# First layer: experts' outputs added to tokens by indirect DMAs, and late modulation blocks put into the routing

## The chip, the cores and the metric

The kernel runs on one core of a Trainium2 chip. The metric is the device time of one execution in microseconds; where several executions were timed, their median stands for the kernel. TensorE multiplies, VectorE and ScalarE work on what it leaves in PSUM, GpSimd does the indirect transfers, and SyncE issues the plain ones. Each engine takes its own instructions in order.

## The reference

Two blocks of a network follow each other on 512 tokens of width 1024. The first block has two layers. Each computes a mixer (convolutions and attention) and then experts; in the first layer 256 context tokens take the same way as the 512 tokens, in the second they are only read. What matters here is the expert part of the first layer:

```
h2    = rms_norm(x, n2) * (1 + sc2) + sh2          # scales and shifts: "modulation", c @ ada_w + ada_b
probs = softmax(h2 @ router)                       # 16 experts
for each expert e:                                 # expert choice: the expert picks its tokens
    its 64 tokens (32 context tokens) with the highest probs[:, e], weights g
    y = (silu(h @ w_gate[e]) * (h @ w_up[e])) @ w_down[e]
    out[tokens] += g * y                           # a token can be picked by several experts
x = x + g2 * out                                   # the context: xc = xc + cg2 * outc
```

All is float32. The weights of one expert are 3 x 4 MB, those of a layer's experts 201 MB.

## The kernel before, in words

Tokens stand transposed in SBUF: `xT` is 128 partitions x 8 x 512 (feature within a block, block, token), `xcT` the same for 256 context tokens. Instructions are written in program order; a planner then sets the order on every engine by a priority (program order) and a cost model, puts in the waits, and gives out the buffers of the pools.

`experts(l, ...)` begins at line 1022; `has` is true in the first layer. Its steps:

Weights. A unit is a tile of 128 rows x 1024 columns (512 KB) of one weight of one expert; the units are taken in the order gate 0, up 0, gate 1, down 0, up 1, gate 2, down 1, ... `wload(n)` issues the next n loads from SyncE. In the first layer there are 18 tiles `rawA`, 5 tiles `raw` (slots "W", from a pool that the modulation blocks and the dense weights share) and 2 tiles `rawB`, in turn: 25 units. Each product that has used up a unit issues the load of the next.

Modulation. `ada_gen(l, blocks, ...)` (lines 309 to 333) computes one block of 512 modulation values from four tiles `raw` of `ada_w`: eight matmuls, a copy, four transposes, a reduction into `M[l]`. It loads three of the four tiles of the block after it in advance. Blocks 8 to 11 of layer 1 are run at line 1158, after the routing in program order.

Routing (lines 1078 to 1168). Root mean squares and router logits, a softmax, then the top-k: eight rounds of three VectorE instructions on `D` (lines 1123 to 1127), which give the tokens and weights of all experts. Beside it TensorE transposes all tokens back to rows, ScalarE scales them, and SyncE writes them to `hd` in memory. At the end `tok` and `gidx` (token numbers) and `gcol` (weights) are there.

Experts. `gather(e)` (line 1177) is an indirect transfer from GpSimd: 96 rows of `hd` (64 tokens, 32 context tokens) into `xg`. `xpose` transposes them and applies the modulation. `run_gu("g")`, `act`, `run_gu("u")`, `mul`, `hpose` and `down` are the products of one expert; they are run so that `down(e - 1)` stands between the gate and up products of expert e. A product of a unit is four matmuls into the columns of four quarters of TensorE for the tokens (partitions 32 g to 32 g + 32: two halves of the 64 tokens, two halves of the 1024 output columns) and four for the context (four quarters of the columns).

Scatter. `down` leaves y in PSUM (`yx`, `yc`). It is weighted and split in two parts (`Yx`, `Yc`: a rounded value and the rest, lines 1298 to 1308). After every fourth expert `scatter(qd)` builds one-hot matrices from `iota` and `tA`, `tC` (lines 1315, 1350), multiplies them with the parts (lines 1328, 1355), so that each token's column sums what was picked for it, and adds the result, times g2, to `xT` and `xcT` (lines 1331, 1357). It stands in the middle of the up product of experts 4, 8 and 12. The last group is scattered in two steps: `scatter_x(3, (0,))`, the tokens of experts 12 and 13, after expert 14 (line 1390), and after the last product the tokens of experts 14 and 15 and the context of experts 12 to 15, with the squares that the next layer's norm needs.

Of the kernel before, what the change touches and what calls it, by code (L numbers as in the profile page):

```python
# [134 lines left out]
def main_kernel(ctx, tc, I, out, stop=None, dbg=None, manual=False):  # L135
# [173 lines left out]
    def ada_gen(l, blocks, pl, psp):  # L309
        g, o, n = RO["adab"]  # L310
        for b in blocks:
            ada_load(l, b)
            p = psp.tile([128, 512], F32, name="misc")
            for hf in range(4):
                r = raws.pop(("ada", l, b, hf)).rearrange("p (k c) -> p k c", k=2)
                for i in range(2):
                    q = (hf % 2) * 2 + i
                    T.matmul(p[32 * q:32 * q + 32, :], lhsT=s2[:, hf * 2 + i, :], rhs=r[:, i, :],
                             start=(hf < 2), stop=(hf >= 2))
            if 3 < b < 11 or (l == 1 and b != 7 and b < 11):  # L320
                ada_load(l, b + 1, hfs=range(3))
            sb = pl.tile([128, 512], F32, name="sq")
            A.activation(sb, p, AF.Copy)
            yield
            p = psp.tile([128, 512], F32, name="misc")
            for j in range(4):
                T.transpose(p[:, 128 * j:128 * j + 128], sb[:, 128 * j:128 * j + 128], ident)
            mm = M[l][:, 4 * b:4 * b + 4, :]
            V.tensor_reduce(mm, p.rearrange("p (j q s) -> p j s q", j=4, q=4)[:, :, 0:2, :], axis=AX.X, op=OP.add)
            V.tensor_tensor(mm, mm, cols[:, g, o + 48 * l + 4 * b:o + 48 * l + 4 * b + 4, None].to_broadcast([128, 4, 2]),  # L330
                            op=OP.add)
            yield
# [8 lines left out]
    if True:  # L341
# [680 lines left out]
        def experts(l, rwpA, lg, rbias, a2, nA, nB):  # L1022
# [35 lines left out]

            wload(nA + 5)
            with ExitStack() as es:  # L1060
                dr = pool(es, "dr", space=DRAM)
                mp = pool(es, "mp")
                ps = pool(es, "ps", space=bass.MemoryType.PSUM)
                hd = dr.tile([NT, 1024], F32)
                tok = mp.tile([128, 48], F32)
                gcol = mp.tile([128, 48], F32)
# [6 lines left out]
                with ExitStack() as e2:  # L1073
                    hp = pool(e2, "hp")
                    sqp = pool(e2, "sqp2", 3)
                    psp = Psum(ps, {"tr": 2}, {"misc": "tr"})
                    r = roots(sqp, tok_sums(psp, [stA], NTT), NTT, 1.0 / 1024)

# [25 lines left out]
                    D = hp.tile([80, 256], F32)  # L1104
                    V.tensor_copy(D[:NP], pd[:NP, 0:256])
                    wload(6 if l else 0)

                    for t in range(NTT):
# [7 lines left out]
                        SY.dma_start(hd[t * 128:(t + 1) * 128, :], ht)  # L1116
                    wload(nB - (6 if l else 0))


                    vals = hp.tile([80, 64], F32)  # L1120
                    idx = hp.tile([80, 64], U32)
                    for i in range(8):
# [3 lines left out]
                        if i < 7:  # L1126
                            V.match_replace(out=D[:NP], in_to_replace=v8, in_values=D[:NP], imm_value=-1.0)
                    tg = hp.tile([80, 128], F32)
                    ti = hp.tile([80, 128], F32)
# [25 lines left out]
                    else:  # L1155
                        V.tensor_copy(gidx[0:64, :], tok[0:64, 0:16])
                if has:
                    drain(ada_gen(1, range(8, 12), mp, Psum(ps, {"yx": 1}, {"misc": "yx"})))

# [66 lines left out]

                def run_gu(w, e, mid):
                    px = ps.tile([128, 512], F32, name=("ax" if w == "g" else "ux"))
                    pc = ps.tile([128, 256], F32, name=("ac" if w == "g" else "uc")) if has else None
                    xt = xsT[e]  # L1230
                    for u in range(8):
# [3 lines left out]
                        if u == 3:  # L1235
                            for m in mid:
                                m()
                    acc[w, e] = (px, pc)

# [15 lines left out]
                def hpose(e):  # L1255
# [11 lines left out]
                    hT[e] = h  # L1267

                def down(e):
                    px = ps.tile([128, 512], F32, name="yx")  # L1270
# [12 lines left out]
                    for u in range(8):  # L1283
                        r = wt.pop(("d", e, u))
                        prod(px, pc, e, u, r, lx, lc, u == 0, u == 7)
                        wload(1)

                    if e % 4 == 0:
                        Y["x", 0] = sp.tile([128, 2, 2, 512], F32R, name="Yx", bufs=2)
                        Y["x", 1] = sp.tile([128, 2, 2, 512], F32R, name="Yx", bufs=2)  # L1290
                        if has:
                            Y["c"] = sp.tile([128, 2, 4, 256], F32R, name="Yc", bufs=1)
                    y = Y["x", (e % 4) // 2]
                    for g in range(2):
                        hf = g ^ (e % 2)
# [15 lines left out]
                def onehots(qd, pr):  # L1311
                    ohs = []
                    for hf in range(2):
                        oh = sp.tile([128, 512], F32R, name="oh", bufs=4)
                        V.tensor_scalar(oh, iota, tA[:, hf, 2 * qd + pr:2 * qd + pr + 1], None, op0=OP.is_equal)
# [57 lines left out]
                for e in range(17):  # L1373
# [7 lines left out]
                    if e < 16:  # L1381
                        mid = [lambda: xpose(e + 1)]
                        if e > 0 and e % 4 == 0:
                            mid.append(lambda: scatter(e // 4 - 1))
                        run_gu("u", e, mid)
                        mul(e)
                        gather(e + 2)
                    if e == 14:
                        scatter_x(3, (0,))
# [504 lines left out]
```

## Time and profile before

| | |
|---|---|
| median of 3 executions | 2691.11 us (2687.1 to 2695.84) |
| the profiled execution | 2693.99 us |
| its span in the profile | 2692.1 us |
| TensorE (PE) busy | 2512.2 us, 93% |
| VectorE (DVE) / ScalarE (ACT) / GpSimd (POOL) busy | 1156.3 / 900.7 / 590.2 us |
| routing and experts of the first layer | about 451 to 1110 us of the span |

The profile is one execution on the chip. Times count from the start of the span. PE is a matmul on TensorE, PEld a weight load of it, which overlaps with matmuls. An instruction group reads: engine, line, operation, output<-inputs. A matmul of float32 appears as two records. "x8" counts instructions; in square brackets stands how long the engine was idle before, and who released it.

### The profile page before, as it was taken

How to read it: one execution, taken by the hardware profiler on the slowest of the kernel's cores; microseconds unless marked ns; L12 is line 12 of the kernel's file. 1: busy time of each engine (PE TensorE's matmuls, PEld its weight loads, DVE VectorE, ACT ScalarE, POOL GpSimd, SP SyncE). 2: the span in 40 equal slices, each digit the busy share in tenths (PEclk: the TensorE clock that was granted, in tenths of full speed). 3: DMA queues.
4: the chain of work that ended last, by engine and by line, in shares of the span. 5: the costliest groups of instructions: out<-in, count | busy, mean ns of one | idle time of the engine just before them, and what ended most of it. 6: DMA issues, size and time to landing. Idle time of an engine off the chain costs nothing.

```text
span 2692.1 us, 41575 instructions
## 1 busy us (share of the span) xinstructions
PE 2512.2 (93%) x16527; PEld 1526.5 (57%) x16527; DVE 1156.3 (43%) x2466; ACT 900.7 (33%) x1831; POOL 590.2 (22%) x495
## 2 busy tenths in 40 slices
PE   7999999799999999799979989898899999999997
PEld 4776687344444444577753322122577787888876
DVE  4488853223222232679741101021665555444411
ACT  4544363111221211455532111110552435444322
POOL 3423111000000000434220000000333233444443
PEclk9999999899999999799989999999999999999999
DMA  8455365799998987122089999999421102333321
GB/s 287 128 168 155 124 220 208 265 393 375 361 392 313 392 313 251 52 58 65 28 308 361 399 395 400 399 404 409 127 63 32 40 25 63 94 100 96 93 87 64
DMA packets 319352, 572.57 MB, mean 213 GB/s; under 512 B 36320, under 2 KB 187927, under 8 KB 318519
## 3 DMA queue, kind: packets, MB, share of 16 engines
q1 hardware_dynamic: 311143, 552.01, 57.1%
q0 software_dynamic: 7872, 17.84, 2.7%
q8 instruction: 130, 2.13, 0.3%
q14 instruction: 63, 0.52, 0.1%
q10 hardware_dynamic: 144, 0.08, 0.0%
HBM read 553.60 MB, written 10.49 MB: 210 GB/s over the span
## 4 chain that ended last, share of the span: by engine, by line
PE 69%; DMA 15%; DVE 9%; POOL 2%; issue 2%; ACT 2%; SPq 1%; ACTq 0%; DVEq 0%; POOLq 0%
PE px L473 20%; PE ux L1215 4%; PE ax L1215 4%; PE yx L1215 4%; DMA rawA<-in_w_down_dram 3%; PE g L473 2%; PE y L584 2%; PE tr L1328 2%; PE s L553 2%; PE ac L1220 2%; PE px L475 2%; PE uc L1220 2%; PE yc L1220 2%; DMA rawA<-in_w_up_dram 2%; PE ux L1209 2%
## 5 line engine op out<-in xcount | busy, mean ns | idle before, releaser
L443 POOL TENSOR_TENSOR wl<-raw,wh 128x512 fp32r<-128x512 f32 (+1 forms) x312 | 409.0, 1314 | 971.5 <-ACT wh L442 779.2
L442 ACT ACTIVATE wh<-raw 128x512 fp32r<-128x512 f32 (+1 forms) x312 | 193.5, 625 | 441.5 <-PE px L473 210.9
L473 PE MATMUL px<-hh,wh 128*128 128x512 f32 x768 | 316.3, 413 | 5.8 <-DVE xT L1331 1.8
L473 PE MATMUL px<-hh,wl 128*128 128x512 f32 x768 | 314.1, 409 | 6.9 <-POOL wl L443 6.9
L473 PE MATMUL px<-hl,wh 128*128 128x512 f32 x768 | 315.6, 411 | 4.9 <-DVE hl L1019 3.1
L1299 DVE SCALAR_TENSOR_TENSOR Yx<-yx,gcol,Yx 64x512 fp32r<-64x512 f32 x64 | 48.0, 749 | 501.4 <-ACT Yx L1298 501.4
L1181 POOL DMA_INDIRECT xg<-hd,gidx x32 | 29.3, 914 | 842.0 <-PE tr L1193 785.5
L473 PEld LDWEIGHTS px<-hh,wl 128*128 128x128 f32 x768 | 149.5, 195 | 40.5 <-POOL wl L443 7.6
L473 PEld LDWEIGHTS px<-hh,wh 128*128 128x128 f32 x768 | 149.2, 194 | 40.4 <-issue 6.1
L473 PEld LDWEIGHTS px<-hl,wh 128*128 128x128 f32 x768 | 149.3, 194 | 38.6 <-issue 3.8
L1197 ACT ACTIVATE xt<-tr,mod,a 128x64 f32<-128x64 f32 x256 | 86.3, 406 | 197.0 <-PE tr L1193 192.9
L1298 ACT ACTIVATE Yx<-yx,gcol 64x512 fp32r<-64x512 f32 x64 | 43.7, 682 | 317.8 <-PE yx L1215 158.6
L1243 ACT ACTIVATE sa<-ax 128x512 f32<-128x512 f32 x32 | 19.1, 598 | 353.8 <-PE ax L1215 240.7
L785 DVE SCALAR_TENSOR_TENSOR yT<-ub,cols,yT 128x512 f32<-128x512 f32 (+1 forms) x180 | 126.6, 720 | 0.6
L1215 PE MATMUL ax<-rawA,xt 128*32 128x512 f32 x856 | 122.3, 603 | 0.0
L1215 PE MATMUL ux<-rawA,xt 128*32 128x512 f32 x800 | 118.6, 595 | 0.0
L1209 PE MATMUL ux<-rawA,xt 128*64 128x512 f32 x328 | 87.3, 611 | 8.1 <-DMA rawA<-in_w_up_dram 7.9
L1209 PE MATMUL yx<-rawA,hT 128*64 128x512 f32 x316 | 81.5, 621 | 11.5 <-DMA rawA<-in_w_down_dram 10.6
L1328 PE MATMUL tr<-oh,Yx 128*128 128x512 f32 x256 | 78.9, 434 | 12.0 <-ACT Yx L1298 8.1
L565 PE MATMUL pt<-tab,P 128*128 128x128 f32 x448 | 82.7, 285 | 6.9 <-DVE PT L571 4.3
L1209 PE MATMUL ax<-rawA,xt 128*64 128x512 f32 x316 | 77.5, 611 | 8.4 <-DMA rawA<-in_w_gate_dram 7.8
L1328 PEld LDWEIGHTS tr<-oh,Yx 128*128 128x128 f32 x256 | 45.7, 196 | 60.4 <-DVE xT L1331 23.6
(578 smaller groups left out, 4912.0 us busy)
## 6 DMA issues: line engine op xcount, KB each, us to landing
rawA<-in_w_gate_dram SPq DMA_DIRECT2D x186, 512.0 KB, 9.3
rawA<-in_w_up_dram SPq DMA_DIRECT2D x182, 512.0 KB, 10.2
rawA<-in_w_down_dram SPq DMA_DIRECT2D x151, 512.0 KB, 10.2
raw<-in_ada_w_dram SPq DMA_DIRECT2D x80, 512.0 KB, 5.8
raw<-in_w_down_dram SPq DMA_DIRECT2D x74, 512.0 KB, 7.4
raw<-in_w_gate_dram SPq DMA_DIRECT2D x62, 512.0 KB, 10.1
raw<-in_w_in_dram SPq DMA_DIRECT2D x56, 512.0 KB, 5.2
raw<-in_w_up_dram SPq DMA_DIRECT2D x55, 512.0 KB, 6.7
```

What stands on the lines that cost most here:

```text
L442: A.activation(wh[:, :n], raw[i][:, a:a + n], AF.Copy)
L443: G.tensor_tensor(wl[:, :n], raw[i][:, a:a + n], wh[:, :n].bitcast(F32), op=OP.subtract)
L473: T.matmul(px, lhsT=w[:, k % 4, :], rhs=h[:, k0 + k, 0:512], start=st, stop=sp_)
L475: T.matmul(pc, lhsT=w[:, k % 4, :], rhs=h[:, k0 + k, 512:nt], start=st, stop=sp_)
L553: T.matmul(s[:, :w], lhsT=q, rhs=k, start=(a == 0), stop=(a == len(mm) - 1))
L565: T.transpose(pt[:, (t - a) * 128:(t - a + 1) * 128], P[:, t * 128:(t + 1) * 128], ident)
L785: V.scalar_tensor_tensor(acc[:, j, o:o + n], src, w, acc[:, j, o:o + n], op0=OP.mult, op1=OP.add)
L1197: A.activation(xt[:, kk, 0:64], p[:, k * NX:k * NX + 64], AF.Identity, bias=M[l][:, 24 + kk, 0:1], scale=a2[:, kk, 0:1])
L1209: T.matmul(px[64 * g:64 * g + 64, :], lhsT=lx(u), rhs=w[:, 512 * hf:512 * hf + 512], start=first, stop=last)
L1215: T.matmul(px[32 * g:32 * g + 32, :], lhsT=lx(u)[:, 32 * (g % 2):32 * (g % 2) + 32], rhs=w[:, 512 * hf:512 * hf + 512], start=first, stop= ...
L1220: T.matmul(pc[32 * g:32 * g + 32, :], lhsT=lc(u), rhs=w[:, 256 * q:256 * q + 256], start=first, stop=last)
L1328: T.matmul(p, lhsT=Y["x", pr][:, hl_, hf, c * 128:(c + 1) * 128], rhs=ohs[pr][hf], start=(n == 0), stop=(n == 2 * len(prs) - 1))
```

## The change

In the first layer (`has`), the scaled outputs of an expert go to memory instead of being scattered by matmuls. Two arrays of sums stand in device memory: `sumx`, 1024 rows x 512 (two rows per token, one for each half of the columns), and `sumc`, 1024 rows x 256 (four rows per context token). They are filled with zeros from a tile, by two DMAs from SyncE after the writes to `hd`. `place` holds for each partition and expert the row: 2 * token + half, or 4 * token + quarter.

- `down(e)` for e < 14: ScalarE scales `yx` into one tile `ys`, and an indirect DMA from GpSimd adds its 128 rows of 2 KB to `sumx`. For e < 12 VectorE scales `yc` into `yt`, whose 128 rows of 1 KB are added to `sumc`. The two-part split, the one-hot matrices and the matmuls of these experts fall away.
- The tokens of experts 14 and 15 and the context of experts 12 to 15 go the old way, after the last product.
- The sums are read back by six DMAs from GpSimd (`sums_load`: a tile `rb` of 128 tokens x 1024, two buffers), issued after the up products of experts 13 (context) and 14. `sums_add(n)` transposes half a tile (four transposes) and adds it, times g2, to `xT` or `xcT` (four VectorE instructions). The four calls for the context stand in the up product of expert 15, the eight for the tokens between the units of `down(15)`.
- Modulation blocks 8 to 11 of layer 1 are taken in steps during the routing: block 8 after the copy into `D`, the other three after rounds 2, 4 and 6 of the top-k. Their next block is now loaded in four tiles in advance, not three. The five units in slots "W" are loaded after the routing, not before it, and the fourth tile of block 8 takes their place.

```diff
-                ada_load(l, b + 1, hfs=range(3))
+                ada_load(l, b + 1, hfs=range(4 if l == 1 and b > 7 else 3))
...
-            wload(nA + 5)
+            wload(nA if has else nA + 5)
+            if has:
+                ada_load(1, 8)
...
+                    accs = dr.tile([1024, 512], F32, name="sumx"), dr.tile([1024, 256], F32, name="sumc")
+                    place = mp.tile([128, 2, 16], I32)
+                    part = mp.tile([128, 2, 16], F32)
...
+                    ga = ada_gen(1, range(8, 12), mp, Psum(ps, {"yx": 1}, {"misc": "yx"})) if has else iter(())
...
+                    for _ in steps(ga, 2):
+                        pass
                     wload(6 if l else 0)
...
                     wload(nB - (6 if l else 0))
+                    if has:
+                        zz = sqp.tile([128, 1024], F32, name="ht", bufs=4)
+                        G.memset(zz, 0.0)
+                        for acc_, n in zip(accs, (512, 256)):
+                            SY.dma_start(acc_.rearrange("(p a) c -> p (a c)", p=128).rearrange("p (b c) -> p b c", c=1024),
+                                         zz[:, None, :].to_broadcast([128, n // 128, 1024]))
...
+                        if i in (2, 4, 6):
+                            for _ in steps(ga, 2):
+                                pass
...
+                wload(5 if has else 0)
                 if has:
-                    drain(ada_gen(1, range(8, 12), mp, Psum(ps, {"yx": 1}, {"misc": "yx"})))
+                    for i, n in enumerate((2.0, 4.0)):
+                        V.scalar_tensor_tensor(part[:, i], tok[:, 32 * i:32 * i + 16], n, part[:, i], op0=OP.mult, op1=OP.add)
+                    V.tensor_copy(place, part)
...
+                        if each and u % 2:
+                            each(8 + u // 2)
...
+                def add_rows(i, e, y):
+                    G.indirect_dma_start(out=accs[i][:, :], out_offset=bass.IndirectOffsetOnAxis(ap=place[:, i, e:e + 1], axis=0),
+                                         in_=y, in_offset=None, compute_op=OP.add)
+
+                rb = {}
+
+                def sums_load(t):
+                    rb[t] = sp.tile([128, 1024], F32, name="rb", bufs=2)
+                    i, t0 = divmod(t, 4)
+                    G.dma_start(rb[t], accs[i].rearrange("(t a) c -> t (a c)", a=(2, 4)[i])[t0 * 128:t0 * 128 + 128, :])
+
+                def sums_add(n):
+
+                    t, hf = divmod(n, 2)
+                    r = rb[t]
+                    x, s, t0 = (xT, 0, t) if t < 4 else (xcT, 1, t - 4)
+                    p = ps.tile([128, 512], F32, name="tr", bufs=2)
+                    for k in range(4):
+                        T.transpose(p[:, k * 128:(k + 1) * 128], r[:, (hf * 4 + k) * 128:(hf * 4 + k + 1) * 128], ident)
+                    for k in range(4):
+                        kk = hf * 4 + k
+                        xv = x[:, kk, t0 * 128:t0 * 128 + 128]
+                        V.scalar_tensor_tensor(xv, p[:, k * 128:(k + 1) * 128], M[l][:, 40 + kk, s:s + 1], xv,
+                                               op0=OP.mult, op1=OP.add)
...
+                        if has and e == 15:
+                            sums_add(u)
+                    if has and e < 14:
+
+                        y = sp.tile([128, 512], F32, name="ys")
+                        A.activation(y, px, AF.Copy, scale=gcol[:, e:e + 1])
+                        add_rows(0, e, y)
+                    if has and e < 12:
+                        y = sp.tile([128, 256], F32, name="yt", bufs=1)
+                        V.tensor_scalar(y, pc, gcol[:, 32 + e:33 + e], None, op0=OP.mult)
+                        add_rows(1, e, y)
+                        return
...
-                        if e > 0 and e % 4 == 0:
+                        if e > 0 and e % 4 == 0 and not has:
                             mid.append(lambda: scatter(e // 4 - 1))
-                        run_gu("u", e, mid)
+                        if has and e == 15:
+                            run_gu("u", e, [], sums_add)
+                        else:
+                            run_gu("u", e, mid)
                         mul(e)
                         gather(e + 2)
-                    if e == 14:
+                        if has and e in (13, 14):
+                            for t in ((4, 5), range(4))[e - 13]:
+                                sums_load(t)
+                    if e == 14 and not has:
                         scatter_x(3, (0,))
```

## Rows read from the trace of the kernel before

**Rows 1.** The page: TensorE's busy time, share and instructions; the chain by engine.

```profile
PE 2512.2 (93%) x16527; PEld 1526.5 (57%) x16527; DVE 1156.3 (43%) x2466; ACT 900.7 (33%) x1831; POOL 590.2 (22%) x495
...
PE 69%; DMA 15%; DVE 9%; POOL 2%; issue 2%; ACT 2%; SPq 1%; ACTq 0%; DVEq 0%; POOLq 0%
```

**Rows 2.** Stretches: length, busy us of PE, PEld, DVE, ACT, POOL, clock, DMA share, GB/s.

```profile
451.00:485.00 34.00, 19.81 (x122) 11.85 (x124) 25.46 (x102) 12.63 (x21) 2.81 (x4) 0.76 0.54 193
512.00:545.00 33.00, 29.35 (x289) 12.06 (x285) 4.38 (x14) 5.01 (x10) 0.00 (x0) 0.95 0.90 318
...
560.00:650.00 90.00, 90.00 (x1094) 37.11 (x1090) 19.54 (x43) 17.54 (x40) 1.82 (x2) 1.00 1.03 400
700.60:799.10 98.50, 98.50 (x1198) 40.83 (x1194) 23.37 (x55) 20.42 (x49) 2.72 (x3) 1.00 1.03 389
799.10:847.90 48.80, 48.49 (x450) 21.91 (x446) 19.84 (x43) 6.87 (x17) 0.91 (x1) 1.00 0.77 281
...
1500.00:1860.00 360.00, 319.86 (x1324) 92.89 (x1324) 60.75 (x90) 49.73 (x121) 7.95 (x9) 1.00 1.03 401
```

**Rows 3.** GpSimd's timeline, the gathers: start and length in us, instruction, idle before.

```profile
503.49 0.91 POOL L1181 DMA_INDIRECT xg<-hd,gidx  x1 [17.89 <-PE tr L1193]
553.24 0.91 POOL L1181 DMA_INDIRECT xg<-hd,gidx  x1 [48.84 <-PE tr L1193]
586.10 0.91 POOL L1181 DMA_INDIRECT xg<-hd,gidx  x1 [31.94 <-PE tr L1193]
...
651.79 0.91 POOL L1181 DMA_INDIRECT xg<-hd,gidx  x1 [31.94 <-PE tr L1193]
700.58 0.91 POOL L1181 DMA_INDIRECT xg<-hd,gidx  x1 [47.87 <-PE tr L1193]
```

**Rows 4.** The chain in order of time: start, us, gate matmuls behind hpose, experts 12 to 15.

```profile
924.60 0.99 PE ax L1215 x8
...
973.39 1.00 PE ax L1215 x8
...
1006.24 0.99 PE ax L1215 x8
...
1045.75 1.00 PE ax L1215 x8
```

**Rows 5.** Timeline around one hpose.

```profile
513.06 0.61 PE L1220 MATMUL ac<-raw,xt 128*32 128x256 f32 x8
...
514.10 0.38 PE L1265 MATMUL tr<-tab,sa 128*128 128x128 f32 x2
...
514.41 1.06 PE L1215 MATMUL ax<-raw,xt 128*32 128x512 f32 x8
```

**Rows 6.** Lines 1331 and 1357: count, duration in ns (min/median/max), first and last start.

```profile
L1331 DVE SCALAR_TENSOR_TENSOR xT<-tr,mod,xT x80: 737/750/752, 655.7 to 1905.0; 128x512 f32<-128x512 f32 x80
...
L1357 DVE SCALAR_TENSOR_TENSOR xcT<-tr,mod,xcT x32: 474/484/485, 666.7 to 1103.3; 128x256 f32<-128x256 f32 x32
```

**Rows 7.** DMA issues, 451 to 485, then 485 to 1070: count, median us to landing.

```profile
xg<-hd,gidx POOLq DMA_INDIRECT x3, 4.6
...
raw<-in_ada_w_dram SPq DMA_DIRECT2D x13, 512.0 KB, 6.8
...
xg<-hd,gidx POOLq DMA_INDIRECT x14, 7.9
```

**Rows 8.** Timeline of the routing: copy into D, first gather, first gate matmuls.

```profile
461.56 0.42 DVE L1105 COPY D<-tr 80x256 f32<-80x256 f32 x1 [1.20 <-PE tr L1103]
...
478.24 1.00 POOL L1181 DMA_INDIRECT xg<-hd,gidx  x1 [25.68 <-DVE tC L1168]
...
484.35 1.94 PE L1215 MATMUL ax<-rawA,xt 128*32 128x512 f32 x8
```

**Rows 9.** Timeline of the layer's end: last "down" matmuls, next layer's first matmul.

```profile
1083.42 0.61 PE L1220 MATMUL yc<-rawA,hT 128*32 128x256 f32 x8
...
1109.72 0.79 PE L473 MATMUL px<-hh,wh 128*128 128x512 f32 x1 [1.17 <-ACT hh L416]
```

More of the change, by code (lines that the diff above doesn't have):

```diff
@@ L1064, in experts @@
                 hd = dr.tile([NT, 1024], F32)
+                if has:
+                    accs = dr.tile([1024, 512], F32, name="sumx"), dr.tile([1024, 256], F32, name="sumc")
+                    place = mp.tile([128, 2, 16], I32)
+                    part = mp.tile([128, 2, 16], F32)
+                    for g in range(4):
+                        pr = slice(32 * g, 32 * g + 32)
+                        for e in range(2):
+                            G.memset(part[pr, 0, e:16:2], float((g // 2) ^ e))
+                        for e in range(4):
+                            G.memset(part[pr, 1, e:16:4], float((g - e) % 4))
                 tok = mp.tile([128, 48], F32)
@@ L1117, in experts @@
                     wload(nB - (6 if l else 0))
+                    if has:
+                        zz = sqp.tile([128, 1024], F32, name="ht", bufs=4)
[3 more added lines that the diff above has]
+                                         zz[:, None, :].to_broadcast([128, n // 128, 1024]))
                     vals = hp.tile([80, 64], F32)
@@ L1225, in experts, with run_gu @@
                 Y = {}
-                def run_gu(w, e, mid):
+                def run_gu(w, e, mid, each=None):
                     px = ps.tile([128, 512], F32, name=("ax" if w == "g" else "ux"))
@@ L1286, in down @@
                         wload(1)
-                    if e % 4 == 0:
+                        if has and e == 15:
[9 more added lines that the diff above has]
+                        return
+                    if has:
+                        if e == 12:
+                            Y["c"] = sp.tile([128, 2, 4, 256], F32R, name="Yc", bufs=1)
+                        elif e == 14:
+                            Y["x", 1] = sp.tile([128, 2, 2, 512], F32R, name="Yx", bufs=1)
+                    elif e % 4 == 0:
                         Y["x", 0] = sp.tile([128, 2, 2, 512], F32R, name="Yx", bufs=2)
                         Y["x", 1] = sp.tile([128, 2, 2, 512], F32R, name="Yx", bufs=2)
[L1291 to L1294, printed above, removed]
+                    for g in range(2 if not has or e > 13 else 0):
+                        y = Y["x", (e % 4) // 2]
                         hf = g ^ (e % 2)
@@ L1313, in onehots @@
                     for hf in range(2):
-                        oh = sp.tile([128, 512], F32R, name="oh", bufs=4)
+                        oh = sp.tile([128, 512], F32R, name="oh", bufs=2 if has else 4)
                         V.tensor_scalar(oh, iota, tA[:, hf, 2 * qd + pr:2 * qd + pr + 1], None, op0=OP.is_equal)
```

## The prediction

> **What bounds the kernel now.** I read the page first: TensorE is busy for 93% of the span and carries 69% of the chain that ended last, transfers 15% [rows 1]. So a microsecond counts if it leaves TensorE's own queue or a wait of that queue. The change touches the router and the experts of the first layer, 451 to 1110 us; I cut that part into stretches [rows 2]. The reader is to see three things there. While the experts run (560 to 650, 700.6 to 799.1) TensorE is busy 100% at full clock, and the transfers are nearly full too: 400 and 389 GB/s at a DMA share of 1.03. While a scatter runs (799.1 to 847.9) the DMA share falls to 0.77. During the routing (451 to 485) TensorE is busy 19.8 of 34 us. In the second layer the weights do set the pace, at 401 GB/s (1500 to 1860): I take 400 GB/s as what the 16 engines give.
>
> Then I went through GpSimd's timeline, because each gather is released by the token transposes of the next expert, so the distance of two gathers is the time of one expert [rows 3]. An expert with nothing beside it takes 32.85 us (553.24 to 586.10; nine such distances). One with a scatter takes 48.79 (651.79 to 700.58; two such distances). The second expert takes 49.75 (503.49 to 553.24): there the modulation blocks 8 to 11 of the next layer stand between its matmuls. The chain gives the rest, from gate matmul to gate matmul: 48.79 us with the third scatter (924.60 to 973.39), 32.85 without (to 1006.24) and 39.51 with the half scatter at e = 14 (to 1045.75) [rows 4].
>
> **What the change takes away.** Three scatters: 3 x (48.79 - 32.85) = 47.8 us. The half scatter: 39.51 - 32.85 = 6.7 us. The modulation blocks among the experts: 49.75 - 32.85 = 16.9 us, work and waits for their loads together (between 512 and 545 us TensorE is idle for 3.65 us [rows 2]). Sum 71.4 us, all of it in TensorE's queue while that was full, so all of it is on the path. The smaller evictions (one ScalarE and one VectorE instruction in place of twelve per expert) save nothing: VectorE is busy 23.4 and ScalarE 20.4 of 98.5 us there [rows 2].
>
> **What it adds.**
> Reading the sums back: 12 calls of sums_add, four transposes each, four in the "up" products of expert 15 and eight in its "down". The six transposes of hpose take 0.92 us of the queue: without them the gate matmuls at 514.41 would follow the context matmuls of 513.06 after 0.43 us, not 1.35 [rows 5]. Four cost about 0.65, so 12 x 0.65 = 7.8 us, on the path. The VectorE side, four adds of 128 columns: 0.75 us for 512 columns and 0.48 for 256 [rows 6] make about 0.35 for 128, 1.4 us a call, under the 1.37 us of a weight tile (32.85 / 24) and its 0.65 of transposes. Hidden.
>
> Waiting for rows read back: rb has two buffers and six tiles pass through them. A load can go when the sum before last is added, some three weight tiles (3 x 2.0 = 6 us) ahead of its use; a GpSimd transfer of 393 KB landed in 4.6 us on quiet queues and 7.9 on full ones [rows 7]. Below, nothing; above, 2 us on each of four tiles; I take 2 us, since the weights are nearly through by then.
>
> The routing: here the experts start at 484.35, released by the gather of 478.24, and VectorE's top-k chain begins with the copy of D at 461.56 [rows 8]. Blocks 8 to 11 are now put into this stretch, with 2.1 MB of loads per block, of which only one and a quarter can be in the five raw tiles at a time; after the hd writes SyncE's queue also issues 3.1 MB of zeros. In this stretch the queues moved 193 GB/s x 34 us = 6.6 MB [rows 2]. Now it is 3.1 (hd) + 6.3 (blocks 9 to 11) + 3.1 (zeros) + 1.0 (two tiles B) + 0.4 to 0.8 (gathers) = 14 to 15 MB, that is 35 us at 400 GB/s. TensorE and VectorE take instructions in order: a modulation step put ahead of its load's landing holds up the top-k steps or the transposes behind it, and so the gather. Below: -2 us (the first gate matmuls, after an idle TensorE, take 1.94 us for eight where later ones take 1.06 [rows 5, 8]; with work ahead of them that may shrink). Above: three loads in a row, each landing in 6.8 us as among the experts [rows 7] and followed by about 2.5 us of matmul, copy and transpose, end at 461 + 3 x 9.3 = 489, and were that ahead of the first gather, it would be 489 - 478 = 11 late. I take +4, nearer the lower end: block 8 and a quarter of 9 are loaded beforehand, and the gather landing on full queues (7.9 for 4.6) alone gives 3.3.
>
> GpSimd's queue: 26 adds of about 0.91 us each (as the gathers issue in [rows 3]) and 24 small memsets. GpSimd is busy 2.7 of 98.5 us, and the next gather behind an add has an expert's time to land. Nothing. The place columns are three small VectorE steps: nothing.
>
> The weights: without scatters the queues lose their pauses. For each expert they move 12.58 MB of weights and 0.39 of gather in 32.85 us, 395 GB/s; the sums add 0.39 MB written (128 rows of 2 KB and 128 of 1 KB), so 407 GB/s against 400. That eats the lead of 25 tiles (34 us, some 10 of them landing time) by 1.8% of 460 us = 8 us, on top of the 11 us that the routing leaves over (its 35 us of traffic against the 24 us from 461 to 485). Below, no stall; above, the lead is gone at the first experts and the 8 us, plus the 13 us that a second pass over the 5.2 MB of all adds would cost, are all paid: 21 us. I take 5.
> The Trainium skill ("DMA: Bandwidth & Descriptors", Rules for kernel authors) says that an accumulating DMA reads its destination and writes it later. By that the need is 419 GB/s and the 13 us would be owed; no transfer in this trace accumulates, so no run so far shows it.
>
> **The sum.** -71.4 + 7.8 + 2 + 4 + 5 = -52.6 us. The profiled execution took 2693.99 us (span 2692.1), 2.9 above the median of 2691.1. So 2641 by the profile, and I forecast **2639 us** as the median. The end of the layer does not change: the last matmul of the sixteenth expert to the next layer's first, 1083.42 to 1109.72 [rows 9], because the scatter of experts 14 and 15 and of context experts 12 to 15 stays. Its own range: the terms at their good ends give -71.4 + 7.8 - 2 = -65.6 (2625); at their middling bad ends (routing +8, loads +12, rb +4) -39.6 (2651). With a few us for the order in which the planner sets 384 tiles, 2620 to 2652.
>
> **Rivals.**
> (a) The weight loads become the bound. For it: the DMA share of 1.03 at 389 GB/s says that little is spare. Against: no TensorE wait for a weight tile stands among these experts now, and the lead is a whole expert. Price: the 21 us in full and 8 at the routing: -71.4 + 7.8 + 2 + 8 + 21 = -32.6, 2658.
> (b) The modulation blocks hold the routing, or the planner leaves them among the experts after all, so that this part does not do what it says. For it: TensorE did wait for such loads among the experts (the 3.65 us). Against: the planner places a step by when it expects its data. Price: 11 in place of 4, or the 16.9 kept and the 4 not paid: 7 to 13 us less gain, 2646 to 2652.
> (c) Slower. An add is not a write of 0.26 MB but holds the 16 engines, since every row must be fetched, added and written back; the weights behind it stand still. 26 adds; the gain of 52.6 and the 5 already counted are gone at 57.6 / 26 = 2.2 us each. If each costs what a gather needs to land on quiet queues, 4.6 us, it is 26 x 4.6 - 57.6 = +62, 2753. For it: nothing in the trace accumulates. Against: 26 adds in 530 us, two queues that take turns; the gathers, of like size, leave the rate at 400 (560 to 650).
> (d) The transfers set the time, so that nothing moves: 2691. From 460 us on there are 188.2 MB of weight tiles beyond the first 25, 2.6 + 1.0 for seven of those, 15.6 of hd, blocks, zeros and read-back sums, 6.3 of gathers and 5.2 of adds, 219 MB in all. Were the queues to give 352 GB/s, they would need until 1083 us, as now. Against: 400 and 401 GB/s over 90 and 360 us [rows 2].
> The Trainium skill (same page, Where 436 GB/s comes from) puts HBM to SBUF for one core at about 358 GB/s. By that the experts would end at 1072, and 2680 would be the time; the trace disagrees with its 400 and 401.
>
> **How the numbers follow.** Forecast 0.62; (a) 0.16; (b) 0.10; (c) 0.08; (d), or bad ends adding up to it, 0.04. What one can tell from no change is 0.3%, 8 us: faster 0.88, same 0.04, slower 0.08. The range takes in the forecast, (b) and (a) with some room: 2618 to 2668; left out are (c), (d) and the worst of (a).
>
> **What would show it.** Gathers 33 us apart from the second expert to the last, without 48.8 us steps; 34 or more says (a). The first gate matmul within 488 +- 3 us; beyond 492, or modulation matmuls among gate matmuls, says (b). No TensorE wait for a weight tile above some us in total; if each add is followed by a dip of the transfer rate and such a wait, (c). The stretch from the first gate matmul to the last "down" matmul 542 us long (599 now). Between "down" matmuls of expert 15, waits for rb of 0 to 4 us. The forecast is wrong if the layer's end also grows, which I hold at 26 us.

## The result, and the profile after

The changed kernel takes 2663.58 us (median of 4 runs, 2661.03 to 2670.31) against 2693.48 (4 runs): ratio 0.990, 95% interval 0.988 to 0.992. The gain is 30 us where 52.6 were forecast. Its profiled execution took 2663.15 us (span 2660.6). On the page, as in [rows 1], TensorE has the same share of the span as before (93%), and transfers carry more of the chain (18% for 15%):

```profile
PE 2472.6 (93%) x16415; PEld 1498.3 (56%) x16415; DVE 1091.2 (41%) x2371; ACT 870.0 (33%) x1769; POOL 637.3 (24%) x552
...
PE 65%; DMA 18%; DVE 9%; issue 3%; POOL 2%; ACT 1%; SPq 1%; ACTq 0%; DVEq 0%; POOLq 0%
```

**Where to measure from.** The routing does not start at the same time in every execution: 457.7 us after the span's start here, 455.1 in the kernel before, 449.4 in one of the experiments (no adds), whose TensorE, SyncE and VectorE instructions up to there are the changed kernel's, in the same order. What makes these 8 us I did not find. So I cut each trace from its own routing's start (TensorE's first `tr<-ones,stA`) at four events: the start of ScalarE's `sa<-ax` of experts 2, 11 and 15 (which follows the end of their gate products and is called gate 2, 11 and 15 from here on) and the next layer's first matmul (`px<-hh,wh`). Lengths in us:

| kernel | to gate 2 | to 11 | to 15 | to next layer | sum |
|---|---|---|---|---|---|
| before | 114.1 | 327.5 | 154.0 | 59.0 | 654.6 |
| changed | 116.6 | 295.7 | 142.4 | 70.0 | 624.6 |
| difference | +2.5 | -31.8 | -11.6 | +11.0 | -30.0 |

The 30 us of the two profiled executions are all in this part. The second stretch gained two whole scatters (31.9 by [rows 3]). The first should have lost 12.9 us (16.9 less the 4 paid), the third 22.6 (one scatter and the half one).

**The routing**, timeline by start, several engines; [rows 8] has the same events of before:

```profile
467.17 0.42 DVE L1119 COPY D<-tr 80x256 f32<-80x256 f32 x1 [1.53 <-PE tr L1117]
...
478.06 0.60 SPq L1138 DMA_DIRECT2D sumx<-ht  x1
478.71 0.71 SPq L1138 DMA_DIRECT2D sumc<-ht  x1
479.51 19.20 SPq L196 DMA_DIRECT2D raw<-in_ada_w_dram  x5
...
483.72 1.00 POOL L1209 DMA_INDIRECT xg<-hd,gidx  x1 [6.66 <-DVE tA L1191]
...
494.88 3.43 PE L318 MATMUL yx<-raw,s 128*32 128x512 f32 x8 [13.95 <-DMA raw<-in_ada_w_dram]
498.24 1.06 PE L1221 MATMUL tr<-tab,xg 96*128 96x96 f32 x5
...
500.79 1.07 PE L1243 MATMUL ax<-rawA,xt 128*32 128x512 f32 x8
...
505.43 1.43 PE L318 MATMUL yx<-raw,s 128*32 128x512 f32 x6
...
508.84 0.62 PE L318 MATMUL yx<-raw,s 128*32 128x512 f32 x2 [1.27 <-DMA raw<-in_ada_w_dram]
```

From the routing's start the first gather is 2.9 us later than before (26.0 for 23.2). But block 10's matmuls stand ahead of expert 0's token transposes in TensorE's queue, and their weight tile was issued behind the `hd` writes and the 3.1 MB of zeros (`sumx`, `sumc`). TensorE, idle for 13.95 us, starts the gate at 500.79, 43.1 us after the routing's start; before it was 29.3. Nor is the gate free of blocks then: all of block 11 stands among expert 0's gate matmuls (505.43, 508.84), with a wait for its tile of 1.27 us. From the first gate matmul to `sa<-ax` expert 0 takes 19.5 us, and 13.9 before. So the changed kernel is 13.8 us late at the gate's start and 5.6 more at its end; the 16.9 us that the blocks had cost between gates 0 and 2 come off that, and 2.5 are left.

**The experts.** GpSimd's timeline, for [rows 3]: two adds and a gather for each expert, gathers 32.85 us apart.

```profile
558.39 0.95 POOL L1209 DMA_INDIRECT xg<-hd,gidx  x1 [2.14 <-PE tr L1221]
585.59 1.57 POOL L1300 DMA_INDIRECT sumx<-ys,place  x1 [26.25 <-ACT ys L1347]
587.46 1.56 POOL L1300 DMA_INDIRECT sumc<-yt,place  x1 [0.30 <-issue]
591.24 0.95 POOL L1209 DMA_INDIRECT xg<-hd,gidx  x1 [2.21 <-PE tr L1221]
```

In stretches, as [rows 2] (length, busy us of PE, PEld, DVE, ACT, POOL, clock, DMA share, GB/s): experts 2 to 11 run without a pause of TensorE, at a full DMA share that now gives 385 GB/s and not 400; behind gate 11 TensorE has pauses.

```profile
558.40:886.90 328.50, 328.50 (x3984) 136.09 (x3980) 49.58 (x131) 43.71 (x111) 40.65 (x31) 1.00 1.03 385
886.90:928.20 41.30, 39.35 (x463) 15.18 (x459) 7.52 (x22) 7.06 (x18) 4.65 (x4) 1.00 1.04 382
```

Gates 11 to 15 (ScalarE's timeline) are 35.33, 36.17, 36.04 and 34.84 us apart, 11.0 more in all than four times 32.85:

```profile
869.95 0.60 ACT L1273 ACTIVATE sa<-ax 128x512 f32<-128x512 f32 x1 [13.38 <-PE ax L1243]
905.28 0.60 ACT L1273 ACTIVATE sa<-ax 128x512 f32<-128x512 f32 x1 [15.86 <-PE ax L1243]
941.45 0.59 ACT L1273 ACTIVATE sa<-ax 128x512 f32<-128x512 f32 x1
977.49 0.59 ACT L1273 ACTIVATE sa<-ax 128x512 f32<-128x512 f32 x1
1012.33 0.60 ACT L1273 ACTIVATE sa<-ax 128x512 f32<-128x512 f32 x1 [19.68 <-PE ax L1243]
```

TensorE's waits between 870 and 1012 us (total, times, longest) explain 2.8 of them:

```profile
PE ax L1243 <- DMA rawA<-in_w_gate_dram: 1.9, 2, 1.1
PE ux L1243 <- DMA rawA<-in_w_up_dram: 0.9, 1, 0.9
```

**The end**, for [rows 9]: one wait for rows read back, and from the last "down" matmul to the next layer 26.3 us, as before.

```profile
1050.52 0.63 PE L1317 MATMUL tr<-tab,rb 128*128 128x128 f32 x4 [1.63 <-DMA rb<-sumx]
...
1055.98 0.61 PE L1248 MATMUL yc<-rawA,hT 128*32 128x256 f32 x8
...
1082.31 0.80 PE L473 MATMUL px<-hh,wh 128*128 128x512 f32 x1 [1.17 <-ACT hh L416]
```

### The profile page after: what moved, and what is told of

Read it like the earlier page. It is cut to its first block, busy times and chain, and to the rows that moved or that the text cites. A ratio compares the mean times of both kernels' runs of the same rounds, so it can differ in the third digit from the quotient of the medians.

```text
span 2660.6 us, 41308 instructions
## 1 busy us (share of the span) xinstructions
PE 2472.6 (93%) x16415; PEld 1498.3 (56%) x16415; DVE 1091.2 (41%) x2371; ACT 870.0 (33%) x1769; POOL 637.3 (24%) x552
## 4 chain that ended last, share of the span: by engine, by line
PE 65%; DMA 18%; DVE 9%; issue 3%; POOL 2%; ACT 1%; SPq 1%; ACTq 0%; DVEq 0%; POOLq 0%
PE px L473 20%; PE ax L1243 4%; DMA rawA<-in_w_down_dram 4%; PE yx L1243 3%; PE ux L1243 3%; PE g L473 2%; DMA rawA<-in_w_up_dram 2%; PE y L584 2%; PE px L475 2%; DMA rawA<-in_w_gate_dram 2%; PE s L553 2%; PE ux L1237 2%; PE pt L565 2%; PE ac L1248 2%; PE ax L1237 2%
## 5 line engine op out<-in xcount | busy, mean ns | idle before, releaser
L1369 DVE SCALAR_TENSOR_TENSOR Yx<-yx,gcol,Yx 64x512 fp32r<-64x512 f32 x36 | 27.0, 750 | 266.9 <-ACT Yx L1368 266.9
L1300 POOL DMA_INDIRECT sumx<-ys,place x14 | 22.0, 1571 | 376.7 <-ACT ys L1347 376.7
L1243 PE MATMUL ux<-rawA,xt 128*32 128x512 f32 x800 | 106.1, 594 | 0.9 <-DMA rawA<-in_w_up_dram 0.9
L1237 PE MATMUL yx<-rawA,hT 128*64 128x512 f32 x316 | 80.7, 610 | 12.6 <-DMA rawA<-in_w_down_dram 11.8
L1368 ACT ACTIVATE Yx<-yx,gcol 64x512 fp32r<-64x512 f32 x36 | 24.6, 682 | 191.1 <-PE yx L1237 139.3
L1228 DVE TENSOR_SCALAR xt<-tr,a,mod 128x32 f32<-128x32 f32 x128 | 39.1, 310 | 114.7 <-ACT xt L1225 114.2
```

Of the source, the lines that this page charges most:

```text
L1237: T.matmul(px[64 * g:64 * g + 64, :], lhsT=lx(u), rhs=w[:, 512 * hf:512 * hf + 512], start=first, stop=last)
L1243: T.matmul(px[32 * g:32 * g + 32, :], lhsT=lx(u)[:, 32 * (g % 2):32 * (g % 2) + 32], rhs=w[:, 512 * hf:512 * hf + 512], start=first, stop= ...
```

## Experiments

Three theories for the 22.6 us that are missing. T1: zeros and block loads stand in front of expert 0. T2: the adds use up the weights' lead, so that experts 12 to 15 wait for loads. T3: the read-back costs TensorE its transposes in full. Their rivals stand with the runs; R3, that the order in TensorE's queue and not the loads makes experts 12 to 15 long, became the important one. Lengths are cut as in the table above (gate 2 is what the expectations call the second or third expert's gate); each ratio is to the kernel before as it was timed beside that run. Four of the kernels were timed once only, and what is said of them goes by the stretches of their traces.

| kernel | us (runs) | ratio to before | to gate 2 | to 11 | to 15 | to next layer | sum |
|---|---|---|---|---|---|---|---|
| adds alone | 2662.9 (4) | 0.991 (0.988 to 0.994) | 115.6 | 301.7 | 141.1 | 71.9 | 630.3 |
| move alone | 2686.6 (10) | 0.998 (0.996 to 0.999) | 109.4 | 327.5 | 154.0 | 58.8 | 649.8 |
| zeros in the routing | 2664.6 (4) | 0.989 (0.986 to 0.992) | 115.1 | 295.6 | 142.1 | 70.3 | 623.1 |
| zeros before it | 2655.9 (4) | 0.987 (0.984 to 0.989) | 110.5 | 295.6 | 142.2 | 72.0 | 620.3 |
| same, adds alone | 2667.7 (1) | | 115.5 | 302.0 | 141.2 | 72.0 | 630.6 |
| same, two blocks moved | 2654.5 (4) | 0.986 (0.984 to 0.988) | 107.4 | 295.6 | 141.6 | 72.3 | 616.9 |
| same, transposes low | 2659.3 (4) | 0.987 (0.985 to 0.989) | 111.1 | 298.2 | 141.9 | 69.8 | 621.0 |
| no adds | 2653.2 (4) | 0.987 (0.984 to 0.989) | 117.7 | 295.6 | 138.7 | 68.3 | 620.4 |
| plain writes | 2658.1 (1) | | 116.3 | 295.6 | 138.7 | 68.3 | 619.0 |
| transposes split | 2711.0 (1) | | 126.5 | 335.8 | 143.2 | 68.3 | 673.8 |
| no read-back | 2651.6 (1) | | 118.6 | 296.1 | 140.5 | 59.5 | 614.7 |

**Adds alone, and the move alone.** The first puts the blocks back, the second makes the same edit the other way round on the kernel before:

```diff
-            wload(nA if has else nA + 5)
-            if has:
-                ada_load(1, 8)
+            wload(nA + 5)
...
-                    for _ in steps(ga, 2):
-                        pass
...
-                wload(5 if has else 0)
                 if has:
+                    drain(ada_gen(1, range(8, 12), mp, Psum(ps, {"yx": 1}, {"misc": "yx"})))
```

> The adds, their zero-fill and the read-back alone; the four late modulation blocks and the order of the first weight loads stand as before the change. Theory T1 (the moved blocks' loads, queued behind the zero-fill, stand in front of expert 0, and TensorE, which takes its work in order, waits for them): the move gave back what it gained, so without it the time is the changed kernel's less 0 to 5 us, 2659 to 2664 us; first gate matmul again near 485 us, the 16.9 us of modulation matmuls back among the gate matmuls. Rival R1 (the prediction's terms: 16.9 gained, 4 paid): 13 us above the changed kernel, 2676 us.

> The moved modulation blocks and load order alone, on the kernel before: no adds, no zero-fill, scatters as before. T1: no zero-fill ahead of the block loads, so they land about 7.5 us sooner (3 MB at 400 GB/s); TensorE waits some 6 us for them instead of 14, and the move gains 16.9 - 12 = 5 us: 2688 us. Rival R1: 13 us gained, 2680 us. Rival R2 (the order of the block matmuls in TensorE's queue costs by itself, whatever the loads): no gain or a loss of up to 5 us, 2693 to 2698 us.

T1 holds for the first stretch. The adds alone give the changed kernel's time within 1 us, though by the stretches they are 5.7 us longer (630.3 for 624.6): they are 1.0 shorter up to gate 2 and 6.0 longer up to gate 11, and their routing starts 6.4 us earlier in the profiled execution. What the 6.0 are is shown below. Alone, the move is worth 4.9 us in this part (649.8 for 654.6) and 4.5 by the medians, not 13. To gate 2 it gains 4.7 by itself and loses 2.5 in the changed kernel: 7.2 us between, about what 3.1 MB take at 400 GB/s (7.8).

**The zero-fill elsewhere.** First at the routing's start, then in the w_out products, both issued by GpSimd:

```diff
-                            SY.dma_start(acc_.rearrange(...), zz[:, None, :].to_broadcast([128, n // 128, 1024]))
+                            G.dma_start(...)    # first: ahead of `r = roots(...)`, the same tile
+                        if has and m == 5:      # then: in ev_o, from a tile of that phase
+                            zz = sqp.tile([128, 512], F32, name="sq")
+                            V.memset(zz, 0.0)
+                            for acc_, n in zip(accs, (8, 4)):
+                                G.dma_start(acc_.rearrange(...), zz[:, None, :].to_broadcast([128, n, 512]))
```

> The changed kernel with the zero-fill issued by GpSimd before the routing, where the transfer rate is lowest (39 GB/s at 440-454 us), in place of SP's queue ahead of the block loads. T1: the wait for the block's weight tile in front of expert 0 falls from 14 us to about 6, and the time by 7 us, to 2656 us. R2: the first gate matmul stays near 500 us and the time within 2 us of 2663.6.

The expected 2656 us was missed. GpSimd's first memset of this part waited 11.09 us for the last w_out products, so the zeros went out at 460 us, beside block 9's load. TensorE's wait in front of expert 0 did shrink, to 2.33 us, but one of 4.70 appeared in the routing:

```profile
460.34 0.74 POOL L1093 DMA_DIRECT2D sumx<-ht  x1 [0.30 <-POOL ht L1091]
461.04 0.75 POOL L1093 DMA_DIRECT2D sumc<-ht  x1
...
472.56 1.92 PE L318 MATMUL yx<-raw,s 128*32 128x512 f32 x4 [4.70 <-DMA raw<-in_ada_w_dram]
...
492.74 3.01 PE L318 MATMUL yx<-raw,s 128*32 128x512 f32 x8 [2.33 <-DMA raw<-in_ada_w_dram]
```

> The changed kernel with the zero-fill issued by GpSimd in the last third of the w_out products (near 435 to 445 us, where the engines moved 39 to 217 GB/s), from a tile of that phase, so that it is done before the routing's transfers begin. T1: the 7.5 us that the zero-fill takes leave the stretch between routing and expert 0: the second expert's gate ends some 7 us sooner after the routing's start than in the changed kernel (109.5 instead of 116.6 us, as with the move alone), the time falls to 2656 us (2653 to 2659). R2: no change, 2663.

Now the zeros leave at 434 us and have landed some 11 us later, before the routing. TensorE waits 2.12 us for the same tile. The median falls by 7.7 us, as T1 said; by the stretches 4.3 of them are in this part (620.3 for 624.6: 6.1 gained up to gate 2, some of it lost again behind gate 15), and the profiled routing starts 5.5 us earlier:

```profile
479.97 3.23 PE L319 MATMUL yx<-raw,s 128*32 128x512 f32 x8 [2.12 <-DMA raw<-in_ada_w_dram]
485.98 1.03 PE L1221 MATMUL tr<-tab,xg 96*128 96x96 f32 x5 [2.78 <-DMA xg<-hd,gidx]
```

> The adds alone with the early zero-fill; modulation blocks and first loads as before the change. With the early zero-fill run it tells what the moved blocks are worth once no zeros stand ahead of them. T1: the third expert's gate ends 114 us after the routing's start, as before the change, against 110.5 with the blocks moved: 3.5 us. Rival (the move is worth its 16.9 us less 4, as predicted): 123 us after the routing's start.

Without zeros in the way the move is worth 5.0 us to gate 2 (110.5 for 115.5). It gives 6.4 us more up to gate 11: with the blocks among the experts that stretch is 302.0, not 295.6, since the lengthening that the next paragraphs are about begins behind gate 9 and not behind 11 or 12. The one time of 2667.7 is 11.8 above, as the sums are by 10.3.

> As the early zero-fill, and only blocks 8 and 9 in the routing; 10 and 11 behind it as before the change. T1: the wait of block 10 in front of expert 0 was a wait for its weight tile; with the queue free of zeros little of it is left, so the place of the last two blocks decides little: within 3 us of the early zero-fill alone, 2653 to 2659 us. R2 (each block's matmuls cost their 4.2 us wherever TensorE isn't waiting, and the idle time of the routing could hold all four): 5 to 8 us slower than the early zero-fill alone.

The medians can't be told apart. To gate 2 two blocks are the better by 3.1 us: the third and the fourth did not pay. Both versions beat the kernel before and the changed one (no run of theirs above 2659.1, none of the changed kernel below 2661.0, which was timed on another occasion).

**No adds, and plain writes.**

```diff
-                        add_rows(0, e, y)        # no adds: these two go
-                        add_rows(1, e, y)
-                                         in_=y, in_offset=None, compute_op=OP.add)
+                                         in_=y, in_offset=None)    # plain writes
```

> The changed kernel without the 26 indirect adds (zero-fill, read-back and everything else stay; the contributions of experts 0 to 13 to the tokens, and of 0 to 11 to the context, are left out). T2 (each expert's two adds take about 2.5 us of all 16 engines, so the lead of the weight loads is used up at expert 12): the gates of experts 12 to 15 end 32.9 us apart again instead of 35 to 36, and the time falls by 8 to 11 us, to 2653 to 2656 us. Rival R3 (the order of the transposes in TensorE's queue makes these experts longer, not the loads): the intervals stay at 35 to 36 us and the time within 2 us of 2663.6.

The time was met, for another reason: in the profiled execution the routing starts 8.3 us earlier, and the whole part is only 4.2 shorter (620.4 for 624.6). Only the interval to gate 12 returns to 32.85; the next three are 36.18, 34.87 and 34.84, 7.3 us too long, with TensorE busy in every one of 140 us (ScalarE's timeline, then the stretch with columns as above):

```profile
862.72 0.60 ACT L1273 ACTIVATE sa<-ax 128x512 f32<-128x512 f32 x1 [13.37 <-PE ax L1243]
895.57 0.60 ACT L1273 ACTIVATE sa<-ax 128x512 f32<-128x512 f32 x1 [13.37 <-PE ax L1243]
931.75 0.59 ACT L1273 ACTIVATE sa<-ax 128x512 f32<-128x512 f32 x1
```

```profile
862.00:1002.00 140.00, 140.00 (x1613) 53.52 (x1605) 24.28 (x62) 22.36 (x54) 1.83 (x2) 1.00 1.01 391
```

So T2 holds for 3.7 of the 11.0 us (142.4 to 138.7), and 7.3 come without late loads: the transposes stand in the same groups, in the same order, with and without the adds. Up to gate 12 the eight token transposes of an expert (`tr<-tab,xg`) come as one run, and so do the six of hpose (`tr<-tab,sa`, [rows 5]); behind it both come singly or in pairs. A run of eight costs 0.92 us (746.56 to 747.91, where 0.43 is the step without it); a pair costs 0.43 (906.10 to 906.96) and a single 0.35 (907.84 to 908.62):

```profile
746.56 0.61 PE L1248 MATMUL uc<-rawA,xt 128*32 128x256 f32 x8
747.10 0.88 PE L1221 MATMUL tr<-tab,xg 96*128 96x96 f32 x8
747.91 1.06 PE L1243 MATMUL ux<-rawA,xt 128*32 128x512 f32 x8
...
906.10 0.61 PE L1248 MATMUL yc<-raw,hT 128*32 128x256 f32 x8
906.64 0.38 PE L1221 MATMUL tr<-tab,xg 96*128 96x96 f32 x2
906.96 1.06 PE L1243 MATMUL ux<-raw,xt 128*32 128x512 f32 x8
907.84 0.61 PE L1248 MATMUL uc<-raw,xt 128*32 128x256 f32 x8
908.38 0.30 PE L1221 MATMUL tr<-tab,xg 96*128 96x96 f32 x1
908.62 1.06 PE L1243 MATMUL ux<-raw,xt 128*32 128x512 f32 x8
...
919.90 0.44 PE L1290 MATMUL tr<-tab,sa 128*128 128x128 f32 x2
...
921.69 0.33 PE L1290 MATMUL tr<-tab,sa 128*128 128x128 f32 x1
```

The count closes. Of hpose a pair costs 0.48 and a single 0.37. Between gates 12 and 13 stand five pairs and three singles of token transposes, and two pairs and two singles of hpose: 4.90 us in place of the 1.84 of two runs, 3.1 more, where 3.3 were measured. The next two intervals come to 1.9 each in the same way, and 2.0 each were measured. In the last of them 1.2 us are not the tokens' but the read-back's: four of its transposes (`tr<-tab,rb`) stand among the gate matmuls of expert 15. So R3's order costs 6.1 us, and the read-back 1.2, ahead of gate 15.

> The changed kernel with the 26 indirect adds as plain indirect writes of the same rows (nothing is summed: the last expert's row overwrites the others'). Tells the price of reading the old rows from that of writing. T4 (an add reads and writes, so it takes twice the engines' time of a write): the software queue's share of the engines falls from 10.7% to about 7% between experts 2 and 11 (3.0% is the gathers'), and the lead lasts longer: experts 12 to 15 lose 9 us instead of 11; 2660 to 2663 us. Rival: share and times as in the changed kernel, the price is that of small packets alone.

Plain writes behave like no adds at all: 138.7 us to gate 15 and 68.3 behind it. So TensorE pays for the adding and not for the writing. T4's share of the engines, 7%, was met; its time was not (2658.1 for 2660 to 2663). The software queue (560 to 880 us: packets, MB, share of the engines' time; landing of an add below) in the changed kernel,

```profile
q0 software_dynamic: 3880, 7.62, 10.4%
...
sumx<-ys,place POOLq DMA_INDIRECT x9, 8.1
```

with plain writes,

```profile
q0 software_dynamic: 2272, 7.47, 7.0%
...
sumx<-ys,place POOLq DMA_INDIRECT x10, 6.9
```

and with gathers alone:

```profile
q0 software_dynamic: 1008, 3.54, 4.0%
```

The writes take 3.0 points, the adds 6.4, though the bytes counted are nearly the same; the adds' packets are 2872 for 1264.

**Transposes split, transposes low.** A priority on the eight token transposes, on the changed kernel and on the version with early zeros and two blocks:

```diff
-                        for k in range(4):
-                            T.transpose(p[:, k * NX:(k + 1) * NX], ...)
+                        with (tc.high_priority(offset=-40) if has else nullcontext()):    # split; low: -60
+                            for k in range(4):
+                                T.transpose(p[:, k * NX:(k + 1) * NX], ...)
```

> The changed kernel with another order of TensorE's work: a priority given to the eight token transposes of an expert makes the planner place them one by one between weight tiles' matmuls in every expert, where it stood them in one run of eight up to expert 11. Transfers and instructions are the same. R3 (a single transpose between two tiles costs 0.40 us, a run of eight 0.85): 8 x 0.40 - 0.85 = 2.35 us more for each of the experts 1 to 11, gates 35.2 us apart instead of 32.85, and 26 us in all, 2690 us. T2 (weight loads set the pace of experts 12 to 15, transposes are hidden beside them): no more than 5 us in all, gates still 32.85 us apart.

T2's reading, that these transposes are hidden, is out, and R3 holds more strongly than it said: the experts are 37.32 us apart, 4.47 more than with a run of eight, and the one time is 47 us longer. TensorE waits for no transfer between 600 and 960 us. The eight stand singly here and, unlike those of experts 13 to 15, also between matmuls of one weight tile:

```profile
600.45 0.30 PE L1222 MATMUL tr<-tab,xg 96*128 96x96 f32 x1
600.68 0.62 PE L1249 MATMUL uc<-rawA,xt 128*32 128x256 f32 x2
...
618.13 0.60 ACT L1274 ACTIVATE sa<-ax 128x512 f32<-128x512 f32 x1 [8.24 <-PE ax L1244]
655.45 0.60 ACT L1274 ACTIVATE sa<-ax 128x512 f32<-128x512 f32 x1 [8.25 <-PE ax L1244]
```

> The early zero-fill with two blocks moved, and a lower priority for the token transposes, which makes the planner keep 25 groups of them where it makes 29. By the 0.4 us that a group costs, 1.5 to 2 us less than with the two blocks moved alone: 2652 to 2654 us; faster than the changed kernel by 9 to 11 us. R3's rival (order of transposes decides nothing): the same as with the two blocks moved, 2654.5 us.

A miss: fewer groups, but experts 3 to 12 came out at 33.1 us instead of 32.85, and the third stretch did not shrink. TensorE's waits between 560 and 900 us show where most of it goes: the gate matmuls wait for the scaled tokens `xt` from ScalarE, 2.4 us in 11 waits, which they do in neither the changed kernel nor the version with two blocks. A count of groups is too coarse a measure of an order.

**No read-back.**

```diff
-                        if has and e == 15:
-                            sums_add(u)
...
-                        if has and e in (13, 14):
-                            for t in ((4, 5), range(4))[e - 13]:
-                                sums_load(t)
```

> The changed kernel without the read-back: its six loads, 48 transposes and 48 adds are left out (what experts 0 to 13, for the context 0 to 11, add to the tokens never reaches them). T3 (each of the 21 insertions of these transposes between weight tiles' matmuls costs 0.4 to 0.67 us of TensorE): from the gate of expert 13 to the next layer's first matmul 10 to 12 us less than in the changed kernel, near 2652 us. Rival (TensorE would wait there for weight tiles or for the last expert's outputs anyway, and the transposes are hidden): 0 to 4 us less, 2660 to 2663 us.

T3 holds: 59.5 us behind gate 15, as before the change (59.0), against 70.0, and 1.9 less before it (140.5 for 142.4): 12.4 us. The changed kernel's trace has the 12 calls in 21 groups. The eight calls for the tokens stand as runs of four, at 0.70 us each; the 16 transposes of the four calls for the context are split into ten singles and three pairs, at 0.37 and 0.48. That is 10.7 us, and the wait for `rb` is 1.63. So the calls are on TensorE's path in full.

## Why the prediction had the direction right and the gain too large

By its own terms, from the routing's start (the order of transposes was no term of it, but a few us in its range):

| term | predicted | measured |
|---|---|---|
| three and a half scatters gone | -54.5 | -54.5 |
| blocks out of the experts, and what the routing pays | -16.9 + 4 | +2.5 |
| the weights' lead | +5 | +3.7 |
| order of the transposes ahead of gate 15 | | +6.1 |
| sums read back, waits for rb | +7.8 + 2 | +12.2 |
| sum | -52.6 | -30.0 |

- **Scatters: right.** Two of them are the 31.8 us of the second stretch; the rest is in the third, where the experts without a scatter are taken as 32.85 us and what is above that stands in the rows below.
- **The routing: mis-sized, 15.4 of the 22.6 us.** The 4 us were meant for the first gather, and that is 2.9 late. The step ended there. It did not ask what stands between the gather and expert 0: block 10's matmuls, ahead in TensorE's queue, whose loads SyncE issues behind `hd` and the zeros. The working had the bytes (14 to 15 MB, 35 us at 400 GB/s) and set them against the gather. Of the 15.4, some 6 are the zeros (116.6 to 110.5 when they go early); most of the rest is block work that the routing's idle time does not hold, since the move alone gains 4.7 and not 12.9. Rival (b) named the place, and both of its signs came: the first gate matmul is past 492, and modulation matmuls stand among the gate matmuls of expert 0. Its price of at most 13 us was too small.
- **The lead: right within 1.3.** Loads that came late cost 3.7 us, the prediction's mechanism, inside its bounds.
- **The order of the transposes: 6.1 us that no term held.** They come without any late load, where the planner's order has single transposes and pairs; the count of these groups and the kernel with all token transposes split show that the order is their cause. The prediction allowed for it only as "a few us" of its range. Why the planner splits them behind gate 12 is open; with the blocks among the experts the lengthening begins behind gate 9. By the prediction's sign, "34 or more says (a)", these experts at 35 to 36 us would have been put down to loads, and that would have been wrong for most of it.
- **The read-back: 9.8 predicted, 12.2 measured.** The 0.65 us for four transposes is right (0.70 for a run of four). But the step took every call as one run, and the four calls for the context cost 5.1 us in 13 groups where 2.6 were counted. The one wait for rb is 1.63. VectorE stayed hidden.
- **Layer end: right**, 26.3 us.
- **Rivals (c) and (d): out.** 26 adds cost 3.7 us up to gate 15 and 1.7 behind it (68.3 to 70.0; this is the wait for rb, which the kernel without adds does not have), 0.2 each and not 2.2. By their 6.4 points the 18 adds between 560 and 880 us took some 20 us of the engines' time, 1.1 each; that TensorE did not wait there puts the rest down to the lead. The Trainium skill ("DMA: Bandwidth & Descriptors", Rules for kernel authors) says that an accumulating DMA reads its destination and writes it later. The traces fit that, with 6.4 points of engine time for adds and 3.0 for plain writes, though their count of bytes shows no second pass. The prediction left that second pass out of its value and had it in its bound.

The measured median lies within the range of 2618 to 2668, 4 us from its end. Nothing cancelled to bring it there: of the 22.6 us that are missing, 15.4 are the routing, 6.1 the order and 2.4 the read-back, and only the lead gave 1.3 back. The range had been drawn to take in (b) and (a), one at a time.

## What to carry to other kernels

When work is moved into a gap, follow the in-order queue of the engine that matters up to the first instruction that counts, not only to the transfer that releases it; and put what it must load, and every fill that nobody needs yet, ahead of the gap. The same 3.1 MB cost at most 1.1 us up to gate 2 when issued at 434 us, where the changed kernel's queues move 50 GB/s (110.5 for 109.4 with no zeros), 4.6 more at 460 (115.1) and 6.1 more at 478 (116.6). Small TensorE operations in a full queue are cheap in runs and dear singly, so look at the order of the finished program before blaming the loads.

## What was not expected of the hardware

- An accumulating scatter of 128 rows holds GpSimd for 1.56 us, of 2 KB or 1 KB alike, a gather of 96 rows 0.95; the estimate was 0.91.
- Adding rows in memory takes over twice the engines' time of writing them (6.4 to 3.0 points), at nearly the same count of bytes.
- A transpose of a 96-row block between matmuls costs 0.35 us alone and about 0.11 in a run of eight (0.92 / 8). Where it also splits a weight tile's matmuls it is 0.67: (4.47 + 0.92) / 8.
